# Seven half products for eight in the gate and up pairs of two SwiGLU layers, on one core

## The chip, the cores and the metric

The kernel runs on one core of one Trainium2 chip. The metric is device time in microseconds (us) of one execution, from the first to the last instruction and what lies around them. Lower is better. Times of the kernel before were taken in three runs.

## The reference, cut to what matters

A block of an encoder works on `x` of 256 rows and 2048 columns in float32: a feed-forward layer (FFN) added at half weight, then attention and retention side by side ("the mixer"), then a second FFN and a final norm.

```python
def swiglu_ffn(x, w_gate, w_up, w_down):
    return (jax.nn.silu(x @ w_gate) * (x @ w_up)) @ w_down
...
    x = x + 0.5 * swiglu_ffn(rmsnorm(x, norm_ffn1_g[l]), ffn1_w_gate[l], ffn1_w_up[l], ffn1_w_down[l])
    h = rmsnorm(x, norm_mix_g[l])
    proj = h @ w_in[l]
...
    x = x + merged @ w_out[l]
    x = x + 0.5 * swiglu_ffn(rmsnorm(x, norm_ffn2_g[l]), ffn2_w_gate[l], ffn2_w_up[l], ffn2_w_down[l])
return rmsnorm(x, norm_final_g)
```

The gate and up matrices are 2048 by 5632, the down matrix 5632 by 2048. Everything is wanted at nearly float32 precision.

## The kernel before, in words

**Precision by splitting.** TensorE multiplies a reduced float32 type (F32R). Each operand is therefore split into a high part, which is the value rounded to that type, and a low part, which is the rest. A product is three matmuls: high by high, high by low, low by high (lines 125 to 127). For weights the split is done on the chip as they arrive: ScalarE casts the tile to the high part (line 107), VectorE subtracts it from the raw tile to get the low part (line 108).

**Chunks.** All weights are read once, in chunks of 256 rows by 512 columns (two k-tiles of 128 rows, `KC = 2`, 512 KB). A chunk meets both row tiles of `x` (128 rows each), so it costs 2 k-tiles x 2 row tiles x 3 = 12 matmuls with 512 columns, one cast and one subtraction, both 128 partitions by 1024 elements. A block of 512 output columns is a `Gemm`: it has two accumulators in PSUM (one for each row tile), runs over its chunks, and at the end calls its `done` function, which takes the accumulators out. The whole kernel is one list of 768 chunks.

**The order.** `run` (line 129) walks the list. At step c it first calls `split_upto` (line 111), which issues the splits of up to a few chunks ahead (five tiles for the high part and five for the low part, `SPLIT_BUFS`), and with each split the load of a later chunk on SyncE's queue (four raw tiles). Then it issues what is due at this step, then the matmuls of chunk c. The order in which Python issues instructions is the order of each engine's queue; an engine does not pass an instruction that waits. So work that is issued behind a waiting instruction on the same engine waits too.

**The FFN** (line 366). There are 11 blocks of 512 columns. For each block the gate `Gemm` (8 chunks) is followed by the up `Gemm` (8 chunks). `gate_done` lets ScalarE apply silu (line 374), `up_done` lets VectorE multiply (line 379), and two steps later `put` transposes the product on TensorE (line 269, eight transposes) and splits it into high and low parts (lines 263 and 264). After six blocks, and again after the other five, the down products follow; `down_done` adds them to `x` on VectorE (line 357). The operand of gate and up is the transposed `x`, split by `Norm.put` (lines 316 to 333); the norm's factor is applied when the accumulators are taken out.

Of the kernel before, what the change touches and what calls it, by code (L numbers as in the profile page):

```python
# [32 lines left out]
SPLIT_BUFS = 5  # L33
ACT_TILES = 26
TAIL = 4
AHEAD = (2, 3)
WARM = (6, 3)
# [3 lines left out]
class Gemm:  # L41


    def __init__(self, w, row0, col0, nk, act, done):
        self.w, self.row0, self.col0, self.nk, self.act, self.done = w, row0, col0, nk, act, done
        self.parts = [(t, slice(0, NB)) for t in range(NT)]


@with_exitstack
def block_kernel(ctx: ExitStack, tc: tile.TileContext, x, g1, w1g, w1u, w1d, gm, w_in, rel, woa, wor, wo,  # L50
# [15 lines left out]
    def acc_tile(name):  # L66
        return psum.tile([P, NB], F32, tag="acc", name=name)

    def side_tile(name):
        return psum.tile([P, NB], F32, tag="side", name=name)  # L70
# [5 lines left out]
    chunks = []  # L76
    state = {"dma": 0, "split": 0, "step": 0}
    raws, splits = {}, {}
    due = {}

    def later(steps, fn):
        due.setdefault(state["step"] + steps, []).append(fn)

    def pieces(c):

        return [slice(j, j + 1) for j in range(KC)] if c == 0 else [slice(0, KC)]

    def load(c):
        job, k = chunks[c]
        t = wpool.tile([P, KC, NB], F32, tag="raw", bufs=RAW_BUFS, name=f"raw{c}")  # L90
        r0 = job.row0 + k * P
        src = job.w[r0 : r0 + KC * P, job.col0 : job.col0 + NB].rearrange("(k p) n -> p k n", p=P)
        for p in pieces(c):
            nc.sync.dma_start(t[:, p, :], src[:, p, :])
        raws[c] = t

    def load_next():
        if state["dma"] < len(chunks):
            load(state["dma"])
            state["dma"] += 1  # L100

    def split(c):
        raw = raws.pop(c)
        hi = wpool.tile([P, KC, NB], F32R, tag="hi", bufs=SPLIT_BUFS, name=f"hi{c}")
        lo = wpool.tile([P, KC, NB], F32R, tag="lo", bufs=SPLIT_BUFS, name=f"lo{c}")
        for p in pieces(c):
            nc.scalar.copy(hi[:, p, :], raw[:, p, :])  # L107
            nc.vector.tensor_sub(lo[:, p, :], raw[:, p, :], hi[:, p, :].bitcast(F32))  # L108
        splits[c] = hi, lo

    def split_upto(n):

        while state["split"] < min(len(chunks), n):
            while state["dma"] < min(len(chunks), state["split"] + RAW_BUFS):
                load_next()
            split(state["split"])
            state["split"] += 1
            load_next()

    def products(job, k, whi, wlo, part):  # L120
        ahi, alo = job.act(k)
        t, cs = job.parts[part]
        ts = slice(t * P, (t + 1) * P)
        acc, first, last = job.acc[part], k == 0, k == job.nk - 1
        nc.tensor.matmul(acc, ahi[:, ts], whi[:, cs], start=first, stop=False)  # L125
        nc.tensor.matmul(acc, ahi[:, ts], wlo[:, cs], start=False, stop=False)  # L126
        nc.tensor.matmul(acc, alo[:, ts], whi[:, cs], start=False, stop=last)  # L127

    def run(tail_done):
        head = len(chunks) - TAIL  # L130
        for c in range(head):
            state["step"] = c
            split_upto(c + min(SPLIT_BUFS, AHEAD[0] + c // AHEAD[1]) if c else 2)
            for fn in due.pop(c, []):
                fn()
            job, k0 = chunks[c]
            if k0 == 0:
                if job is chunks[-1][0]:
                    job.parts = TAIL_PARTS
                job.acc = [acc_tile(f"acc{c}_{t}") for t in range(NT)]  # L140
                job.acc += [side_tile(f"acc{c}_{t}") for t in range(NT, len(job.parts))]
                job.acc = [a[:, : cs.stop - cs.start] for a, (t, cs) in zip(job.acc, job.parts)]
            whi, wlo = splits.pop(c)
            for j in range(KC):
                for part in range(len(job.parts)):
                    products(job, k0 + j, whi[:, j, :], wlo[:, j, :], part)
            if k0 + KC == job.nk:
                job.done(job.acc)

        split_upto(len(chunks))  # L150
# [3 lines left out]
        for part, (t, cs) in enumerate(TAIL_PARTS):  # L154
            for c in range(head, len(chunks)):
                job, k0 = chunks[c]
                whi, wlo = splits[c]
                for j in range(KC):
                    products(job, k0 + j, whi[:, j, :], wlo[:, j, :], part)
            tail_done(job.acc[part], t, cs)  # L160
# [111 lines left out]
    class Operand:  # L272
# [18 lines left out]
        def __call__(self, k):  # L291
            return self.hi[k // 4][:, k % 4, :], self.lo[k // 4][:, k % 4, :]

    class Norm:


        def __init__(self, name, gain):
            self.name = name
            self.op = Operand(name, D // NB)
# [34 lines left out]

        def scale(self, t):
            return self.rstd[:, t : t + 1]

    def x_updated(norm):


# [7 lines left out]
    def add(jobs):  # L348
        for job in jobs:
            for k in range(0, job.nk, KC):  # L350
                chunks.append((job, k))
# [431 lines left out]
```

## Time and profile before

| | |
|---|---|
| median of three runs | 2179.64 us (2179.56 to 2180.44) |
| the profiled execution, whole | 2180.46 us |
| its span, first to last instruction | 2178.4 us |
| mean granted clock of TensorE | 0.999 |
| moved by DMA | 414.51 MB, mean 190 GB/s |

The profile is one execution. "Busy" of an engine is the time in which at least one of its instructions was under way. The lines of the profile name the kernel's line, the engine (PE is TensorE, PEld its weight load, DVE is VectorE, ACT is ScalarE, POOL is GpSimd, SP is SyncE), the operation, what is written from what, and shapes. A line of the grouped view ends with the total and mean duration and with the idle time of that engine just before these instructions and who ended it. In the view in order of time a line starts with the start and the duration in us; several like instructions in a row are one line with their count, and its duration is from the start of the first to the end of the last.

### The profile page before, as it was taken

What the parts mean: (1) busy time and instruction counts of PE and PEld (TensorE: products, weight loads), DVE (VectorE), ACT (ScalarE), POOL (GpSimd) and SP (SyncE); (2) the same over time, 40 slices, a digit from 0 to 9 for tenths busy, and PEclk for the clock granted to TensorE, in tenths of its full rate; (3) what the DMA queues carried; (4) which work ended last, traced back from release to release, by engine and by line L of the source; (5) the groups of instructions that cost most, each with busy time, mean ns of one, the idle gap of its engine ahead of it and who ended that gap; (6) DMA issues with size and microseconds to landing.
All of it is one profiled execution on the core that took longest, in us unless ns stands there. A gap on an engine that the chain in (4) does not pass through costs nothing.

```text
span 2178.4 us, 25308 instructions
## 1 busy us (share of the span) xinstructions
PE 2167.7 (100%) x9865; PEld 1802.5 (83%) x9865; DVE 1121.6 (51%) x1192; ACT 963.0 (44%) x1104; POOL 21.6 (1%) x36
## 2 busy tenths in 40 slices
PE   9999999999999999999999999999999999999998
PEld 7888888888888888888888888888888888888887
DVE  5544554445545544556655555554544544444554
ACT  6444433444444444454444444454444433444443
POOL 0000000000000000000000000000000000000000
PEclk9999999999999999999999999999999999999999
DMA  7655655666665555555555555556656556666554
GB/s 253 208 188 187 222 192 194 212 188 190 187 209 184 184 190 187 175 163 178 167 177 190 188 192 192 185 183 194 193 184 193 189 194 212 189 192 191 186 192 137
DMA packets 213512, 414.51 MB, mean 190 GB/s; under 512 B 12864, under 2 KB 13616, under 8 KB 213392
## 3 DMA queue, kind: packets, MB, share of 16 engines
q1 hardware_dynamic: 211424, 406.90, 57.9%
q0 software_dynamic: 1824, 5.93, 0.9%
q8 instruction: 77, 1.26, 0.2%
q14 instruction: 43, 0.35, 0.0%
q10 hardware_dynamic: 144, 0.07, 0.0%
HBM read 409.17 MB, written 3.67 MB: 190 GB/s over the span
## 4 chain that ended last, share of the span: by engine, by line
PE 99%; issue 0%; DMA 0%; ACT 0%; DVE 0%; POOL 0%; POOLq 0%; ACTq 0%
PE acc L125 32%; PE acc L126 32%; PE acc L127 32%; PE f2a0p L269 0%; PE f1a0p L269 0%; PE n1p L322 0%; DMA grows<-in_norm_ffn_g_dram 0%; PE f2a6p L269 0%; PE f1a6p L269 0%; PE mgp L269 0%; PE nmp L322 0%; PE n2p L322 0%; PE as L479 0%; PE rs L537 0%; PE av L514 0%
## 5 line engine op out<-in xcount | busy, mean ns | idle before, releaser
L108 DVE TENSOR_TENSOR lo<-raw,hi 128x1024 fp32r<-128x1024 f32 (+1 forms) x769 | 938.8, 1223 | 1014.0 <-ACT hi L107 1013.6
L107 ACT CAST hi<-raw 128x1024 fp32r<-128x1024 f32 (+1 forms) x769 | 808.2, 1052 | 1106.8 <-PE acc L127 1081.8
L125 PE MATMUL acc<-hi,nmh 128*128 128x512 f32 x704 | 277.8, 395 | 0.0
L125 PE MATMUL acc<-hi,n1h 128*128 128x512 f32 x704 | 276.2, 392 | 0.0
L125 PE MATMUL acc<-hi,n2h 128*128 128x512 f32 x704 | 274.8, 390 | 0.0
L126 PE MATMUL acc<-lo,n1h 128*128 128x512 f32 x704 | 274.7, 390 | 0.0
L127 PE MATMUL acc<-hi,n1l 128*128 128x512 f32 x704 | 274.6, 390 | 0.0
L127 PE MATMUL acc<-hi,nml 128*128 128x512 f32 x704 | 274.5, 390 | 0.0
L126 PE MATMUL acc<-lo,nmh 128*128 128x512 f32 x704 | 274.1, 389 | 0.0
L127 PE MATMUL acc<-hi,n2l 128*128 128x512 f32 x704 | 274.0, 389 | 0.0
L126 PE MATMUL acc<-lo,n2h 128*128 128x512 f32 x704 | 273.9, 389 | 0.0
L127 PEld LDWEIGHTS acc<-hi,n1l 128*128 128x128 f32 x704 | 132.4, 188 | 27.6
L127 PEld LDWEIGHTS acc<-hi,nml 128*128 128x128 f32 x704 | 132.2, 188 | 27.9
L125 PEld LDWEIGHTS acc<-hi,n1h 128*128 128x128 f32 x704 | 132.6, 188 | 27.3
L126 PEld LDWEIGHTS acc<-lo,n1h 128*128 128x128 f32 x704 | 132.4, 188 | 27.3 <-DVE lo L108 0.4
L127 PEld LDWEIGHTS acc<-hi,n2l 128*128 128x128 f32 x704 | 132.2, 188 | 27.5
L126 PEld LDWEIGHTS acc<-lo,n2h 128*128 128x128 f32 x704 | 132.2, 188 | 27.1
L125 PEld LDWEIGHTS acc<-hi,n2h 128*128 128x128 f32 x704 | 132.2, 188 | 27.0
L126 PEld LDWEIGHTS acc<-lo,nmh 128*128 128x128 f32 x704 | 132.3, 188 | 26.2
L125 PEld LDWEIGHTS acc<-hi,nmh 128*128 128x128 f32 x704 | 132.3, 188 | 26.2
L125 PE MATMUL acc<-hi,f2a0h 128*128 128x512 f32 x192 | 74.8, 390 | 0.0
L125 PE MATMUL acc<-hi,f1a0h 128*128 128x512 f32 x192 | 74.8, 389 | 0.0
(266 smaller groups left out, 2107.3 us busy)
## 6 DMA issues: line engine op xcount, KB each, us to landing
raw<-in_ffn_w_up_dram SPq DMA_DIRECT2D x176, 512.0 KB, 3.5
raw<-in_ffn_w_down_dram SPq DMA_DIRECT2D x176, 512.0 KB, 3.6
raw<-in_w_in_dram SPq DMA_DIRECT2D x176, 512.0 KB, 3.5
raw<-in_ffn_w_gate_dram SPq DMA_DIRECT2D x175, 512.0 KB, 3.5
raw<-in_w_out_dram SPq DMA_DIRECT2D x32, 512.0 KB, 3.7
raw<-in_w_out_att_dram SPq DMA_DIRECT2D x16, 512.0 KB, 4.3
raw<-in_w_out_ret_dram SPq DMA_DIRECT2D x16, 512.0 KB, 4.3
xall<-in_x_dram SPq DMA_DIRECT2D x3, 512.0 KB, 7.5
```

What stands on the lines that cost most here:

```text
L107: nc.scalar.copy(hi[:, p, :], raw[:, p, :])
L108: nc.vector.tensor_sub(lo[:, p, :], raw[:, p, :], hi[:, p, :].bitcast(F32))
L125: nc.tensor.matmul(acc, ahi[:, ts], whi[:, cs], start=first, stop=False)
L126: nc.tensor.matmul(acc, ahi[:, ts], wlo[:, cs], start=False, stop=False)
L127: nc.tensor.matmul(acc, alo[:, ts], whi[:, cs], start=False, stop=last)
```

## The change

In both FFNs block 0 stays as it was. For blocks 1 to 10 gate and up are taken as one product of 2 x 2 blocks: `x` is cut into two row tiles (t = 0, 1) and two halves of its columns (8 k-tiles each), and the weights into gate and up, each in the same two halves of rows. The plain way takes eight half products (2 row tiles x 2 column halves x 2 matrices) of 8 k-tiles x 3 = 24 matmuls. The change uses Strassen's scheme in Winograd's form: seven half products, some of them of sums of operands.

The sums of `x` (four, called s3, s5, s6, s7) are made once for each norm, on VectorE, and split like the rest (`add_up`). The sums of weights are made as the weights arrive, on VectorE, in place. A group (one gate and up pair) has 16 steps in four phases of four; a step takes 256 rows of a half:

- phase 0 (p steps): load gate and up of half 0; one sum; two splits; 12 matmuls, into banks a and c;
- phase 1 (q steps): load up of half 1; one sum; two splits; 12 matmuls, into a (with the sum first) and c;
- phase 2 (r steps): load gate of half 1; two sums; two splits; 12 matmuls, into a (with the sum first) and b;
- phase 3 (s steps): no load; one split (of the last sum); 6 matmuls, into a.

Bank a is read out between phases while it goes on accumulating. At the end of phase 0 ScalarE copies a and c; at the end of phase 1 it copies a, and VectorE adds c to that copy; at the end of phase 2 VectorE adds a and b to the copies of phase 0, ScalarE applies silu and VectorE multiplies; at the end of phase 3 ScalarE applies silu to a, and VectorE multiplies.

Between the steps stand plain chunks ("D"), eight in a group and thirteen in the last: up of block 0, then down products, which now run two blocks at a time. The order of a group is `WOVEN`. Eight plain chunks (gate of block 0) stand before the first group and eleven behind the last. Tiles for high and low parts become four each; a p, q or r step takes two of them, an s step or a plain chunk one, and a step is issued ahead only while four suffice. Loads of gate and up of half 0 go into eight tiles of their own (`KEPT`).

The diff, cut to its core:

```diff
 RAW_BUFS = 4
-SPLIT_BUFS = 5
-ACT_TILES = 26
-TAIL = 4
+SPLIT_BUFS = 4
+KEPT = 8
+ACT_TILES = 30
+TAIL = 2
 AHEAD = (2, 3)
+BY_DMA = ()
+HALF_K = D // P // 2
+LEAD = 8
+EARLY = 3
+WOVEN = "ppppD" "ppDppD" "pDpDpDpD" "ssssD"
+WOVEN_LAST = "pDppDpD" "pDpDpDpD" "pDpDpDpD" "ssDssD"
...
+    def prep_upto(n, c):
+
+        while state["prep"] < min(len(steps), n):
+            s = steps[state["prep"]]
+            if s.slots > state["slots"]:
+                return
+            load_some()
...
+            state["slots"] -= s.slots
+            s.prep()
+            for ring in s.frees:
+                room[ring] += 1
+            state["prep"] += 1
+            load_some()
...
         for c in range(head):
             state["step"] = c
-            split_upto(c + min(SPLIT_BUFS, AHEAD[0] + c // AHEAD[1]) if c else 2)
+            prep_upto(c + min(SPLIT_BUFS, AHEAD[0] + c // AHEAD[1]) if c else 2, c)
             for fn in due.pop(c, []):
                 fn()
...
+            steps[c].products()
+            state["slots"] += steps[c].slots
...
+        def add_up(self, p, n):
+
+            if n == 0:
...
+                s5, s7, s6, s3 = self.f
+                nc.vector.tensor_sub(s5, a22, a21)
+                nc.vector.tensor_sub(s7, a11, a21)
+                nc.vector.scalar_tensor_tensor(s6, s5, -1.0, a11, op0=ALU.mult, op1=ALU.subtract)
+                nc.vector.scalar_tensor_tensor(s3, s6, -1.0, a12, op0=ALU.mult, op1=ALU.subtract)
+            for i in (2 * n, 2 * n + 1):
+                self.split_to(self.SUMS[i], slice(4 * p, 4 * p + 4), self.f[i])
...
+            def two(first, second):
+
+                tiles = []
+                for i, raw in enumerate((first, second)):
+                    hi = wpool.tile([P, KC, NB], F32R, tag="hi", bufs=SPLIT_BUFS, name=f"hi{name}{i}")
+                    lo = wpool.tile([P, KC, NB], F32R, tag="lo", bufs=SPLIT_BUFS, name=f"lo{name}{i}")
+                    nc.scalar.copy(hi, raw)
+                    tiles.append((raw, hi, lo))
+                for raw, hi, lo in tiles:
+                    nc.vector.tensor_sub(lo, raw, hi.bitcast(F32))
+                return [(hi, lo) for _, hi, lo in tiles]
+
+            def prep():
+                x = self.x[jc]
+                if phase == 0:
+                    if "T1" not in BY_DMA:
+                        nc.vector.tensor_add(x, x, self.kept[jc])
+                    made["w"] = two(self.kept[jc], x)
+                elif phase == 1:
+                    raw = made["raw"]
+                    if "T2" not in BY_DMA:
+                        nc.vector.tensor_add(x, x, raw)
+                    made["w"] = two(raw, x)
+                elif phase == 2:
+                    raw, k = made.pop("raw"), self.kept.pop(jc)
+                    nc.vector.tensor_sub(k, x, k)
...
+                        nc.vector.tensor_add(x, x, raw)
+                    made["w"] = two(raw, k)
+                else:
+                    made["w"] = [split(self.x.pop(jc), name)]
+
+            def products():
+                w = made["w"]
+                if phase == 0:
+                    self.product("a", "a00", jc, w[0], True, False)
+                    self.product("c", "s5", jc, w[1], True, False)
+                elif phase == 1:
+                    self.product("a", "s6", jc, w[1], False, False)
+                    self.product("c", "s3", jc, w[0], False, True)
+                elif phase == 2:
+                    self.product("a", "s7", jc, w[1], False, False)
+                    self.product("b", "a01", jc, w[0], True, True)
+                else:
+                    self.product("a", "a11", jc, w[0], False, True)
+                if jc == n - 1:
+                    self.end(phase)
...
+            if phase == 0:
+                copied("s1", "a", norm.scale(0))
+                copied("s5", "c", norm.minus_scale(1))
+            elif phase == 1:
+                copied("s2", "a", norm.minus_scale(0))
+                r = copy["s2"]
+                nc.vector.scalar_tensor_tensor(r, acc["c"], norm.minus_scale(0), r, op0=ALU.mult, op1=ALU.add)
+                self.evict(0, 1, r)
+            elif phase == 2:
+                r = copy["s5"]
+                nc.vector.scalar_tensor_tensor(r, acc["a"], norm.minus_scale(1), r, op0=ALU.mult, op1=ALU.add)
+                self.evict(1, 1, r)
+                r = copy["s1"]
+                nc.vector.scalar_tensor_tensor(r, acc["b"], norm.scale(0), r, op0=ALU.mult, op1=ALU.add)
+                self.evict(0, 0, r)
+            else:
+                self.evict(1, 0, None, acc["a"])
...
+            def evict(t, side, r, acc=None):
+                if side == 1:
+                    got["up", t] = r
+                    return
+                if acc is not None:
+                    r = tmp_tile(f"{name}h{b}{t}", "scaled", 2)
+                    nc.scalar.activation(r, acc, AF.Silu, scale=norm.scale(t))
+                else:
+                    nc.scalar.activation(r, r, AF.Silu)
+                nc.vector.tensor_mul(r, r, got.pop(("up", t)))
+                got[t] = r
+                if 0 in got and 1 in got:
+                    later(2, lambda: put_mid(b, got))
```

`copied` is an activation of ScalarE that copies a bank of PSUM to SBUF with the norm's factor; `three` issues the three matmuls of one product; `split` is the cast and the subtraction of before; `room` counts free raw and kept tiles, and `load_some` issues loads in order while the next one has room.

More of the change, by code (lines that the diff above doesn't have):

```diff
@@ L77, in block_kernel @@
-    state = {"dma": 0, "split": 0, "step": 0}
-    raws, splits = {}, {}
+    steps = []
+    transfers = []
+    state = {"dma": 0, "prep": 0, "step": 0}
+    room = {"raw": RAW_BUFS, "kept": KEPT}
     due = {}
[L81 to L93, printed above, removed]
-            nc.sync.dma_start(t[:, p, :], src[:, p, :])
-        raws[c] = t
@@ L108, in split @@
             nc.vector.tensor_sub(lo[:, p, :], raw[:, p, :], hi[:, p, :].bitcast(F32))
[L109 to L127, printed above, removed]
+        return hi, lo
```

339 lines of the change are left out of this document (249 added, 90 removed).

## The prediction

> **What bounds the kernel now.** First the page: busy times, the clock row and the chain that ended last.
>
> ```profile
> PE 2167.7 (100%) x9865; PEld 1802.5 (83%) x9865; DVE 1121.6 (51%) x1192; ACT 963.0 (44%) x1104; POOL 21.6 (1%) x36
> ...
> PEclk9999999999999999999999999999999999999999
> ...
> PE 99%; issue 0%; DMA 0%; ACT 0%; DVE 0%; POOL 0%; POOLq 0%; ACTq 0%
> ```
>
> TensorE (PE) is never without work and makes up 99% of the chain. So what counts is how far its instructions stand apart, and which engine would be next. Second, the groups by line, for who waits for whom:
>
> ```profile
> L108 DVE TENSOR_TENSOR lo<-raw,hi 128x1024 fp32r<-128x1024 f32 (+1 forms) x769 | 938.8, 1223 | 1014.0 <-ACT hi L107 1013.6
> L107 ACT CAST hi<-raw 128x1024 fp32r<-128x1024 f32 (+1 forms) x769 | 808.2, 1052 | 1106.8 <-PE acc L127 1081.8
> ```
>
> ScalarE's cast waits for TensorE to give back a tile, VectorE's subtraction for the cast: both run behind TensorE with slack. Third, the order of time around 303 us (ScalarE, then VectorE), and one pair's stretch with its transposes:
>
> ```profile
> 302.77 1.05 ACT L107 CAST hi<-raw 128x1024 fp32r<-128x1024 f32 x1 [1.67 <-PE acc L127]
> 305.49 1.05 ACT L107 CAST hi<-raw 128x1024 fp32r<-128x1024 f32 x1 [1.67 <-PE acc L127]
> ```
> ```profile
> 303.86 1.22 DVE L108 TENSOR_TENSOR lo<-raw,hi 128x1024 fp32r<-128x1024 f32 x1 [1.50 <-ACT hi L107]
> 306.58 1.22 DVE L108 TENSOR_TENSOR lo<-raw,hi 128x1024 fp32r<-128x1024 f32 x1 [1.50 <-ACT hi L107]
> ```
> ```profile
> 149.53:193.94 44.41, 44.41 (x202) 36.86 (x201) 22.12 (x20) 19.10 (x20) 0.00 (x0) 1.00 0.60 190
> ```
> ```profile
> 149.53 0.87 PE f1a0p L269 x8
> 193.94 0.87 PE f1a0p L269 x8
> ```
>
> One chunk passes every 305.49 - 302.77 = 2.72 us. That is 12 matmuls, so one takes 0.2267 us. The third block is a row of busy times by stretch (length, then busy time and count of PE, PEld, VectorE, ScalarE and POOL, clock, DMA share and rate), the fourth two lines of the chain. A pair of 16 chunks takes 16 x 2.72 + 0.87 (eight transposes) = 44.39 us, and the row says 44.41. In it VectorE is busy 22.12 us, half. The hop from ScalarE to VectorE is 303.86 - (302.77 + 1.05) = 0.04 us.
>
> **What VectorE and ScalarE take when they are not idle.** The change sends VectorE more than it has slack for, so I need the spacing of its instructions back to back. Five rows of the order of time, VectorE first:
>
> ```profile
> 38.77 4.63 DVE L108 TENSOR_TENSOR lo<-raw,hi 128x1024 fp32r<-128x1024 f32 x4 [3.15 <-ACT hi L107]
> ...
> 56.66 1.40 DVE L379 SCALAR_TENSOR_TENSOR f1g<-acc,n1rstd,f1g 128x512 f32<-128x512 f32 x2
> ```
> ```profile
> 313.16 1.28 DVE L357 SCALAR_TENSOR_TENSOR xall<-acc,xall 128x512 f32<-128x512 f32 x2
> ```
> ```profile
> 1151.85 0.69 DVE L613 TENSOR_TENSOR sigr<-sigr,siga 128x512 f32<-128x512 f32 x1
> 1152.46 0.68 DVE L612 TENSOR_TENSOR sigr<-acc,sigr 128x512 f32<-128x512 f32 x1
> ```
> ```profile
> 37.69 2.95 ACT L107 CAST hi<-raw 128x1024 fp32r<-128x1024 f32 x3
> ```
> ```profile
> 213.24 1.37 ACT L374 ACTIVATE f1g<-acc,n1rstd 128x512 f32<-128x512 f32 x2 [0.98 <-PE acc L127]
> ```
>
> Four subtractions of 1024 elements: (4.63 - 1.22) / 3 = 1.137 us apart, each done 1.22 us after its start. With 512 elements: 0.61 us (1152.46 - 1151.85); the x update about 0.60 (half of 1.28, less the overlap); the form with a scale per row 0.66 (1.40 less about 0.74 for the last). Casts of 1024 stand (2.95 - 1.05) / 2 = 0.95 apart; the copy of a bank takes about 0.69. The trace has no float32 sum of 1024 elements from SBUF to SBUF. The add at line 613 is that operation at 512 and has the spacing of its neighbours, so I take 1.137 for the sums, with 1.22 (nothing overlaps) as the upper bound and nothing below it, since 1024 / 512 of 0.61 is already 1.22.
>
> The Trainium skill ("VectorE: DVE Perf Modes", "The DRAIN you can't avoid") has it that the next VectorE instruction does not start until the pipe of the one before is empty; by that every instruction would cost its full 1.22 us, and the sum below is 4.5 us a group more (a rival, below). The same section says that an instruction that is not held starts earlier, and with that this trace agrees: 1.137 against 1.22.
>
> **The sum for one regular group** (16 steps and 8 plain chunks), of which each FFN has nine. Before, the same work is 24 chunks: 24 x 2.72 + 0.87 = 66.2 us.
>
> *TensorE.* Seven half products of 24 matmuls and 8 x 12: 264 x 0.2267 + 0.87 = 60.7 us. It gains 24 x 0.2267 = 5.4 us, in all 20 groups 109 us, if it stays the bound.
>
> *VectorE.* A p or q step has one sum and two subtractions, an r step two and two, an s step one subtraction, a plain chunk one: 8 x 3 + 4 x 4 + 4 + 8 = 52 instructions x 1.137 = 59.1 us. Small ones: three with a scale at ends of phases (2.0), two silu multiplies (1.2), two x updates for each of two down blocks (2.4), two subtractions behind the transposes (1.2): 6.8 us. Together 65.9 us. So VectorE becomes the bound, with as much work as the group took before. The best this can do is to leave the time as it was.
>
> *Where VectorE's queue stands still.* With four tiles, the next step can be split only while TensorE works on the present one, and TensorE begins a step just when VectorE has finished it. The waits that follow, with a step of 2.72 us:
> - p and q steps: sum done at 1.22, hop 0.04, cast 1.05, hop 0.04 = 2.35, while VectorE has two instructions, 2.27. Eight times 0.08 = 0.7 us.
> - End of phase 0: the copies of banks a and c are issued ahead of the casts of the first q step. The last p step ends about 1.5 us after VectorE left it (its second half is 6 x 0.2267 = 1.36 and starts with VectorE's last result); the copies take 1.37, the cast 1.05, the hops 0.1: 4.0 us, against two instructions in hand (2.3). Wait 1.7 us.
> - End of phase 1: VectorE's add of bank c comes behind the last q step (2.72), the copy of a (0.69) and hops (0.1): 3.5 us, and it has one instruction to do in that time (1.14). Wait 2.4 us. Behind it the first r step's four instructions are queued, and TensorE has only one plain chunk (2.72) for the 6 us from its last q step to the first r step's operands (0.7 + 0.1 + 0.66 + 4 x 1.14): it stands still some 3 us. In the middle of this phase one cast waits for a step to end, 0.4 us.
> - End of phase 2: two instructions in hand (2.27) against a step and a hop (2.8): 0.5 us. The multiply comes right behind the silu of ScalarE: 0.1 (the add's own end) + 0.69 + 0.1 (hops) = 0.9 us. The next cast is behind the silu: 0.4 us.
> - End of phase 3: nothing; VectorE is behind by then (five short steps), and TensorE, not VectorE, has the slack.
>
> Sum 7.0 us. A regular group takes 65.9 + 7.0 = 72.9 us, 6.7 more than before. Between the ends (0, if the queue is never late; 9.7, if every wait is 40% longer) I take the worked value, as each step of it has a row.
>
> *The last group* has 13 plain chunks. Before: 29 x 2.72 + 0.87 = 79.8. After: TensorE 324 x 0.2267 + 0.87 = 74.3, VectorE 57 x 1.137 + 8.0 = 72.8 and some 4 of waits: 77. It gains 2.8 us.
>
> *The rest.* Eight plain chunks before and eleven behind the groups cost as before. At the start and before the second FFN VectorE makes the sums of x and splits them, 16 x 0.61 = 9.8 us more, ScalarE about as much:
>
> ```profile
> 0.00:50.00 50.00, 47.09 (x213) 39.33 (x214) 27.42 (x37) 33.42 (x56) 2.46 (x9) 1.00 0.75 255
> ```
>
> VectorE and ScalarE have 23 and 17 us free there; what is late costs perhaps 3 us each time (0 to 10): +6. The mixer and the tail keep their work. Loads:
>
> ```profile
> raw<-in_ffn_w_up_dram SPq DMA_DIRECT2D x176, 512.0 KB, 3.5
> ```
>
> They are as many as before, 24 in a longer group, and land in 3.5 us. The kept tiles come free from the first r step on, over 10 us before they are needed. I cost them at nothing; their cover is that lead, and without it a late load costs up to 3.5 us.
>
> Total, against the profiled execution (2180.5 us with what lies around its span, 0.8 above the median): 18 x 6.7 = +121, 2 x -2.8 = -6, +6: **2301 us**.
>
> **The rivals.**
>
> *The queue is never late (not slower).* If ScalarE and TensorE always answer before VectorE asks, a group takes VectorE's 65.9: 18 x -0.3 - 2 x 5.5 (TensorE's 74.3 in the last groups) + 6 = -10, so 2170 us. It decides at 0.3 us of waits a group. For it: every s step and plain chunk gives VectorE time to get ahead. Against it: four tiles are two steps, and three phase ends put a wait on TensorE's last matmul into VectorE's queue.
>
> *TensorE stays the bound.* 18 x -5.5 - 11 + 6 = -104: 2076 us. It needs (60.7 - 6.8) / 52 = 1.04 us for an instruction of VectorE; the x4 row says 1.137.
>
> *Nothing overlaps on VectorE.* If each instruction started only when the one before is done, 52 x (1.223 - 1.137) = 4.5 us a group and 4.9 in the last: +90, 2391 us. The x4 row speaks against it, unless sums are held where subtractions are not; line 613, which needs the result of the multiply just ahead of it, is the kind that could be.
>
> *The clock drops in the gaps.* The end of the trace shows it:
>
> ```profile
> 2170.00:2172.00 2.00, 0.62 (x6) 0.42 (x4) 1.06 (x3) 0.51 (x2) 0.00 (x0) 1.00 0.76 272
> 2172.00:2174.00 2.00, 0.00 (x0) 0.00 (x0) 0.88 (x2) 1.33 (x2) 0.55 (x1) 0.63 0.02 7
> 2174.00:2178.40 4.40, 0.00 (x0) 0.00 (x0) 0.00 (x0) 0.00 (x0) 0.00 (x0) 0.50 0.64 235
> ```
>
> The last matmul ends at 2170.6; a mean of 0.63 over two microseconds is full clock for 0.5 us and half clock after that, so it fell 1.9 us behind the last matmul. The gap before the first r step is about 3 us, and its step at half clock takes 5.4 instead of 2.7, with VectorE's next cast waiting for its end: 2.7 x 20 = +54, 2355 us. Against it: the other gaps are under 2 us, and how long the clock stays low is not seen. The Trainium skill ("TensorE: Matmul & The Clock Gate", Part 1) lets the clock fall after a whole idle window of about 3.4 us that runs free of the kernel; by that these gaps would keep the clock.
>
> **How the numbers follow.** The forecast (VectorE the bound, 4 to 10 us of waits a group) has 0.74, the clock 0.14, the queue never late 0.06, nothing overlaps 0.04, TensorE the bound 0.02. The forecast's own range is 18 x 2.7 = 49 us to each side, 2252 to 2350; with the clock's case the range is 2250 to 2360, which holds 8 in 10. A measurement of this kernel can tell about 0.2% (4 us) from no change. Faster takes TensorE's case and most of the late-free one, 0.06; the same 0.02; slower 0.92.
>
> **What would show it.** Right: the transposes of the FFN's products stand about 73 us apart; in the groups VectorE is busy about 90% and TensorE waits for L108-like subtractions; the waits of VectorE on the bank copies and on silu stand where I put them, with TensorE's longest gap before the first r step; sums of 1024 elements stand 1.14 us from the next instruction. Wrong: TensorE without gaps in the groups, groups of 61 to 66 us, sums closer than 1.04 us or as far apart as 1.22, a granted clock under 0.97, or casts that wait for loads.

## The result, and the profile after

The changed kernel took 2303.9 us (median of four runs, 2301.5 to 2305.2), the kernel before 2179.6 (2179.3 to 2180.4): 1.057 times the time, interval 1.055 to 1.0587. The profiled execution has a span of 2302.8 us, against 2178.4 before: 124.4 us more.

The page of the changed kernel: busy times, two rows of the 40 slices, the chain, two groups of lines.

```profile
PE 2146.3 (93%) x9337; PEld 1714.8 (74%) x9337; DVE 1836.1 (80%) x1910; ACT 1239.7 (54%) x1468; POOL 21.6 (1%) x36
...
DVE  5999999999999754555655555679999999999997
...
PEclk8999999999999999999999999999999999999999
...
PE 54%; DVE 27%; issue 7%; ACT 6%; DMA 6%; SPq 0%; ACTq 0%; DVEq 0%; POOL 0%; POOLq 0%
...
L115 DVE TENSOR_TENSOR lo<-raw,hi 128x1024 fp32r<-128x1024 f32 (+1 forms) x449 | 545.8, 1220 | 312.1 <-ACT hi L114 311.5
...
L501 DVE TENSOR_TENSOR loz<-rawz,hiz 128x1024 fp32r<-128x1024 f32 x160 | 195.1, 1219 | 22.4 <-ACT hiz L498 22.4
```

The row of slices tells the story. In both FFNs VectorE stands at nine tenths; in the mixer, which the change leaves alone, it is at four to six as before. In the chain VectorE now has 27% where it had nothing. The two groups show why: the plain subtraction (line 115) still had 312 us of idle time before it, nearly all of it in the mixer; the same subtraction in a Strassen step (line 501) had 22 in all. There the cast is ready before VectorE is.

Three groups as stretches (length, then busy time and count of PE, PEld, VectorE, ScalarE and POOL, clock, DMA share and rate), each from the first product into bank a to the next group's; and, as a check, four lines of the chain in order of time, the pair of x updates on which each group ends:

```profile
485.60:557.18 71.58, 65.40 (x275) 50.82 (x274) 67.23 (x65) 40.11 (x43) 0.00 (x0) 0.98 0.53 176
557.18:628.76 71.58, 65.40 (x275) 50.80 (x274) 67.25 (x65) 40.10 (x43) 0.00 (x0) 0.98 0.53 176
628.76:700.35 71.59, 64.10 (x276) 49.59 (x274) 67.25 (x64) 40.41 (x44) 1.52 (x2) 1.00 0.55 185
```

```profile
413.38 1.28 DVE xall L587 x2
484.98 1.28 DVE xall L587 x2
556.57 1.28 DVE xall L587 x2
628.15 1.28 DVE xall L587 x2
```

Both say 71.6 us a group, where the prediction had 72.9 and the work took 66.2 before. VectorE is busy 67.25 of the 71.58 and idle 4.33; TensorE's 264 products and 8 transposes would fit into 60.7.

Where the 124.4 us came from, by the first matmul of each part in the two traces: the 18 regular groups +104.2 (1298.2 us, against 1194.0 for the same 432 chunks before, 66.3 for 24 of them; most groups took 71.6, the first three 75.8, 74.0 and 73.5); the start until the first group +12.3; the same place in the second FFN 0.0; the two last groups with the eleven chunks behind them +3.7 and +1.2; the mixer +1.1; what lies behind the last matmul +1.9. The sum is 124.4.

Now VectorE in one group, in order of time (start, duration, instruction, and in brackets the idle time before it and who ended it):

```profile
570.76 1.22 DVE L513 TENSOR_TENSOR z176x<-z176x,rawz 128x1024 f32<-128x1024 f32 x1
572.99 1.23 DVE L501 TENSOR_TENSOR loz<-rawz,hiz 128x1024 fp32r<-128x1024 f32 x1 [1.01 <-ACT hiz L498]
...
575.26 1.22 DVE L513 TENSOR_TENSOR z176x<-z176x,rawz 128x1024 f32<-128x1024 f32 x1
576.40 1.22 DVE L501 TENSOR_TENSOR loz<-rawz,hiz 128x1024 fp32r<-128x1024 f32 x1
577.68 1.22 DVE L501 TENSOR_TENSOR loz<-z176x,hiz 128x1024 fp32r<-128x1024 f32 x1
...
587.08 1.22 DVE L115 TENSOR_TENSOR lo<-raw,hi 128x1024 fp32r<-128x1024 f32 x1
590.11 0.75 DVE L561 SCALAR_TENSOR_TENSOR z176s<-z176c,n1minus,z176s 128x512 f32<-128x512 f32 x1 [1.81 <-PE z176c L124]
590.78 1.22 DVE L517 TENSOR_TENSOR z176k<-z176x,z176k 128x1024 f32<-128x1024 f32 x1
592.03 1.22 DVE L521 TENSOR_TENSOR z176x<-z176x,rawz 128x1024 f32<-128x1024 f32 x1
...
618.50 0.69 DVE L636 TENSOR_TENSOR z176s<-z176s,z176s 128x512 f32<-128x512 f32 x1 [0.70 <-ACT z176s L635]
619.44 3.50 DVE L115 TENSOR_TENSOR loz<-z176x,hiz 128x1024 fp32r<-128x1024 f32 x3 [0.25 <-ACT hiz L114]
```

Every wait stands at the end of a phase: 1.01 us where phase 0's banks are copied ahead of the first q step's cast, 1.81 where phase 1's bank c is added, 0.70 and 0.25 around the silu. Between the sum at 575.26 and the next instruction lie 1.14 us, the spacing that the prediction took from the subtractions. Between line 517 and line 521 lie 1.25: the second sum of an r step overwrites a tile (z176x) that the first one reads, and it starts only when that one is done.

TensorE around the first r step of that group, and at the kernel's start:

```profile
593.18 0.50 PE L122 MATMUL z176a<-hiz,n1s7h 128*128 128x512 f32 x1 [0.47 <-ACT hiz L498]
595.58 0.50 PE L123 MATMUL z176a<-loz,n1s7h 128*128 128x512 f32 x1 [1.89 <-DVE loz L501]
```

```profile
36.37 1.09 PE L386 MATMUL n1p<-id_sb,xall 128*128 128x128 f32 x4 [8.84 <-DMA xall<-in_x_dram]
```

TensorE's gap before the r steps is there, cut in two by one matmul, which needs only the high part and was ready early. The 8.84 us at the start are new: a transpose waits for the last quarter of `x`.

### The profile page after: what moved, and what is told of

It is laid out like the page before. It is cut to its first block, busy times and chain, and to the rows that moved or that the text cites. A ratio compares the mean times of both kernels' runs of the same rounds, so it can differ in the third digit from the quotient of the medians.

```text
span 2302.8 us, 25403 instructions
## 1 busy us (share of the span) xinstructions
PE 2146.3 (93%) x9337; PEld 1714.8 (74%) x9337; DVE 1836.1 (80%) x1910; ACT 1239.7 (54%) x1468; POOL 21.6 (1%) x36
## 4 chain that ended last, share of the span: by engine, by line
PE 54%; DVE 27%; issue 7%; ACT 6%; DMA 6%; SPq 0%; ACTq 0%; DVEq 0%; POOL 0%; POOLq 0%
PE acc L122 12%; PE acc L123 12%; PE acc L124 12%; DVE loz L501 8%; ACT hiz L498 4%; DVE lo L115 3%; DVE xall L587 2%; DMA raw<-in_ffn_w_down_dram 2%; DVE loz L115 1%; DMA xall<-in_x_dram 1%; DMA z536x<-in_ffn_w_up_dram 0%; DMA rawz<-in_ffn_w_up_dram 0%; ACT hi L114 0%; PE z8a L123 0%; SPq L108 0%
## 5 line engine op out<-in xcount | busy, mean ns | idle before, releaser
L115 DVE TENSOR_TENSOR lo<-raw,hi 128x1024 fp32r<-128x1024 f32 (+1 forms) x449 | 545.8, 1220 | 312.1 <-ACT hi L114 311.5
L114 ACT CAST hi<-raw 128x1024 fp32r<-128x1024 f32 (+1 forms) x449 | 469.7, 1047 | 343.1 <-PE acc L124 312.6
L501 DVE TENSOR_TENSOR loz<-rawz,hiz 128x1024 fp32r<-128x1024 f32 x160 | 195.1, 1219 | 22.4 <-ACT hiz L498 22.4
L498 ACT CAST hiz<-rawz 128x1024 fp32r<-128x1024 f32 x160 | 167.1, 1045 | 55.3 <-issue 28.4
L122 PE MATMUL acc<-hi,nma00h 128*128 128x512 f32 x176 | 70.6, 401 | 0.0
L122 PE MATMUL acc<-hi,nma01h 128*128 128x512 f32 x176 | 70.1, 398 | 0.0
L124 PE MATMUL acc<-hi,nma00l 128*128 128x512 f32 x176 | 68.7, 390 | 0.0
L124 PE MATMUL acc<-hi,nma01l 128*128 128x512 f32 x176 | 68.6, 390 | 0.0
L122 PE MATMUL acc<-hi,nma10h 128*128 128x512 f32 x176 | 68.6, 390 | 0.0
L123 PE MATMUL acc<-lo,nma00h 128*128 128x512 f32 x176 | 68.6, 390 | 0.0
```

The lines of the kernel that those rows point to most:

```text
L122: nc.tensor.matmul(acc, ahi, whi, start=first, stop=False, **more)
L123: nc.tensor.matmul(acc, ahi, wlo, start=False, stop=False, **more)
L124: nc.tensor.matmul(acc, alo, whi, start=False, stop=last, **more)
L498: nc.scalar.copy(hi, raw)
L501: nc.vector.tensor_sub(lo, raw, hi.bitcast(F32))
```

## The experiments

The theory: a group takes VectorE's own work, 65.9 us, and the waits that the ends of phases put into its queue; what is left of the loss arises at the start, where a load is late. Rivals: the loss comes from the clock, from late loads within the groups, or from the order of the steps rather than from VectorE's load.

**e1: without the sums of weights.** All 16 sums of a group are left out.

```diff
-                        nc.vector.tensor_add(x, x, self.kept[jc])
+                        pass
...
-                        nc.vector.tensor_add(x, x, raw)
+                        pass
...
-                    nc.vector.tensor_sub(k, x, k)
...
-                        nc.vector.tensor_add(x, x, raw)
+                        pass
```

> The sixteen sums of weight tiles of each group are left out (VectorE issues none of them; the products then use the plain tiles, so the result is not the reference's). Theory (VectorE is the bound, 52 x 1.137 + 6.8 + 5.7 of waits = 71.6 us a group as measured): VectorE's work falls to 36 x 1.137 + 6.8 = 47.7 us, under TensorE's 60.7, and a group takes 61 to 65 us, somewhat over 60.7 because four tiles still allow only two steps ahead. The whole: 2304 - 20 x 6.6 to 10.6 = 2090 to 2170 us. Rival (the four tiles, the bank copies and the order of the steps hold TensorE up, and VectorE only looks busy): the group stays at 68 us or more, the whole over 2230 us.

Measured: 2140.5 us, 0.9823 of before (0.9808 to 0.9837). One group as a stretch:

```profile
434.78:497.55 62.77, 61.59 (x275) 50.23 (x273) 49.62 (x48) 41.02 (x44) 0.00 (x0) 1.00 0.61 201
```

The group fell by 8.8 us to 62.8, 163 us over the kernel. TensorE is busy 61.59 of it, so it is the bound again; steps, order and banks are as they were. The sums are shown to be the cause. Leaving them out also spares a cast the wait for its sum, but the rows of the changed kernel put that wait at 0.14 us a step (577.68 - 576.40 = 1.28 us, less 1.14), and VectorE at 67.25 us of work in 71.58; it is the time of the sums that counts. The run also shows what is left of TensorE's 109 us in this order of steps, with the start as it is, even if the sums were free: 39.

**e2: the end of a phase one step later.** The copies and adds at a phase's end are issued one step later, so that VectorE meets them when the banks are done.

```diff
-                    self.end(phase)
+                    later(1, lambda: self.end(phase))
```

> The end of each phase (bank copies, adds of banks, silu, multiply) is issued one step later, behind the splits that are issued at that step and ahead of the next step's matmuls. Nothing is left out. Theory (these ends put waits into VectorE's queue, 1.0 us at the end of phase 0, 1.9 at phase 1, 1.2 at phase 2): about 3 to 4 us a group go, 60 to 80 us in all: 2225 to 2245 us. Rival (VectorE's work alone sets the group, and its waits come back elsewhere, at the tiles): 2290 us or more.

Measured: 2257.8 us, 1.0361 (1.0345 to 1.0376). One group, and VectorE where it had waited 1.81 us:

```profile
470.43:539.71 69.28, 63.80 (x274) 49.63 (x272) 67.27 (x64) 40.25 (x44) 0.00 (x0) 1.00 0.56 182
```

```profile
506.08 1.22 DVE L115 TENSOR_TENSOR lo<-raw,hi 128x1024 fp32r<-128x1024 f32 x1
507.22 0.75 DVE L561 SCALAR_TENSOR_TENSOR z152s<-z152c,n1minus,z152s 128x512 f32<-128x512 f32 x1
507.88 1.22 DVE L517 TENSOR_TENSOR z152k<-z152x,z152k 128x1024 f32<-128x1024 f32 x1
```

The wait at the end of phase 1 is gone. A group is 2.3 us shorter, less than I expected: the two waits that it could remove held 1.01 + 1.81 = 2.8 us, and VectorE's own work did not shrink (busy 67.27, as before the edit). So these waits are shown to be some two fifths of the 5.4 us that a group had lost; with them gone VectorE is still busy for 67.27 of 69.28 us.

**e3: the last quarter of x loaded first.** In the changed kernel it is issued at step 2, behind loads of weights that `load_some` may issue much further ahead now.

```diff
     load_x(2 * NB, 3 * NB)
+    load_x(3 * NB, 4 * NB)
...
-    at(2, lambda: load_x(3 * NB, 4 * NB))
```

> The load of the last quarter of x is issued at the start, before the weight loads of the first group, and not at step 2 behind eight of them. Nothing is left out. Theory (TensorE's gap of 9.0 us at 27 us of the profile is that load, queued behind 4 MB of weights): 8 to 12 us less, 2292 to 2296 us. Rival (the gap is the late sums of x, and would only move): under 3 us less.

Measured: 2295.3 us, 1.0532 (1.0515 to 1.055): 8.6 us less, with groups as long as before (71.56). The transposes of the last quarter now follow without a gap:

```profile
26.80 0.60 PE L386 MATMUL n1p<-id_sb,xall 128*128 128x128 f32 x4
...
31.05 0.60 PE L386 MATMUL n1p<-id_sb,xall 128*128 128x128 f32 x4
```

**e8: e2 and e3 together.**

> Both of the earlier edits together: the ends of the phases one step later, and the last quarter of x loaded first. Nothing is left out. Theory: they act at different places (in the groups, before the groups) and add up: 2304 - 46 - 9 = 2249 us (2245 to 2253). Rival (x first only moves the start, and the group's waits come back): 2258 us or more.

Measured: 2253.2 us, 1.0339 (1.0322 to 1.0356), a group of 69.28. The two edits nearly add: 2303.9 - 46.1 - 8.6 = 2249.2, 4 us below the measurement. With both, 74 us of loss are left, 18 x 3.1 = 56 of them in the regular groups, where VectorE is all but full. The next six runs try to give that work to somebody else.

**e4: three of four sums by DMA.** The kernel has a switch, `BY_DMA`, that lets a DMA on GpSimd's queue add one tile to another.

```diff
-BY_DMA = ()
+BY_DMA = ("T1", "T2", "T4")
```

> Twelve of the sixteen sums of weight tiles of a group are made by accumulating DMAs that GpSimd issues, four stay on VectorE. Nothing is left out. Theory (VectorE is the bound): VectorE's work falls by 12 x 1.137 = 13.6 us to 52.3, TensorE's 60.7 is the bound if the DMAs are in time, a group takes 61 to 66 us, the whole 2090 to 2190 us, about the kernel before or under it. Rival (a sum of 512 KB by DMA takes too long or takes the engines of the loads away, 53% busy now): TensorE waits for sums, the group is longer than 71.6 us, the whole over 2304 us.

Measured: 2481.9 us, 1.1402 (1.1371 to 1.1434). One group; GpSimd's queue; VectorE behind it:

```profile
548.16:629.84 81.68, 68.16 (x275) 53.29 (x274) 53.81 (x52) 40.43 (x44) 10.30 (x12) 0.90 0.85 229
```

```profile
693.52 0.86 POOL L478 DMA_DIRECT2D z200x<-z200k  x1 [12.15 <-DMA z200x<-in_ffn_w_up_dram]
694.10 1.16 POOL L519 DMA_DIRECT2D z176x<-rawz  x1
...
705.92 1.22 DVE L115 TENSOR_TENSOR loz<-z176x,hiz 128x1024 fp32r<-128x1024 f32 x1 [11.15 <-ACT hiz L114]
```

VectorE's busy time fell to 53.8 us of a group, and the group still became 10 longer. Line 478, the sum of the *next* group's p step (z200), waited 12.15 us for its weights; the sum that this group's s step needs (line 519, z176) stood behind it in the same queue, and VectorE then waited 11.15 us, for a cast that waited for that sum. An engine's queue is as much a resource as its time. The DMA share rose from 0.53 to 0.85 besides, and the granted clock fell to 0.90; what each of these cost was not separated.

**e9: one of four sums by DMA**, the second sum of an r step, on top of e8.

```diff
-BY_DMA = ()
+BY_DMA = ("T4",)
```

> As the kernel before in this list, with the second sum of each r step made by an accumulating DMA issued by GpSimd (four of sixteen; it is needed only in the s steps). Nothing is left out. Theory (VectorE's work sets the group; the twelve sums by DMA failed because sums with a short deadline came late and blocked the queue for the others): four instructions of 1.137 us less, a group 69.3 - 4.5 = 64.8 us, the whole 2249 - 90 = 2159 us (2150 to 2185), under the kernel before. Rival (accumulating DMAs hinder VectorE or the loads whatever their deadline): 2249 us or more.

Measured: 2220.2 us, 1.019 (1.0173 to 1.0208), 33 less than e8. One group, then ScalarE and VectorE at one point of it:

```profile
523.25:590.76 67.51, 62.88 (x273) 49.85 (x272) 62.34 (x59) 39.78 (x44) 3.39 (x4) 1.00 0.72 215
```

```profile
576.00 1.05 ACT L114 CAST hi<-raw 128x1024 fp32r<-128x1024 f32 x1 [2.46 <-DMA raw<-in_ffn_w_down_dram]
```

```profile
577.08 1.23 DVE L115 TENSOR_TENSOR lo<-raw,hi 128x1024 fp32r<-128x1024 f32 x1 [2.28 <-ACT hi L114]
```

VectorE lost 5 us of work (62.34 instead of 67.27), and the group got 1.8 shorter. The rest went to waits that had not been there, two of VectorE's for a cast, 3.2 us together: the DMA share is 0.72, and one cast waited 2.46 us for a load of `w_down`. So the run lies between the theory and its rival.

**e10: two of four sums by DMA**, the sum of the p step as well, issued at most three steps ahead so that it does not block the queue.

```diff
-BY_DMA = ("T4",)
+BY_DMA = ("T1", "T4")
...
-                if "T1" in BY_DMA:
-                    nc.gpsimd.dma_start(self.x[jc], self.kept[jc], accum_op=ALU.add)
...
+            def sum_first():
+                if jc not in self.x:
+                    return False
+                nc.gpsimd.dma_start(self.x[jc], self.kept[jc], accum_op=ALU.add)
+                return True
...
-                        early if phase == 1 and "T2" in BY_DMA else None)
+                        sum_first if phase == 0 else None)
```

> As the kernel before in this list, with the sum of the p steps by an accumulating DMA as well, issued up to three steps ahead (eight of sixteen). Nothing is left out. Theory: VectorE has 56.8 us of work, the group falls to the 62.7 us that it took without any sum, the whole to 2249 - 20 x 6.6 = 2117 us (2110 to 2150). Rival (a sum by DMA takes 7 us and p steps follow every 3 us, one queue does them in turn): p steps wait, the whole is longer than with one sum by DMA by 20 us or more.

Measured: 2311.2 us, 1.0604 (1.0584 to 1.0624). One group, the chain, and a cast of ScalarE:

```profile
626.48:698.91 72.43, 65.60 (x273) 51.63 (x272) 58.05 (x55) 40.23 (x43) 5.99 (x7) 0.95 0.82 233
```

```profile
PE 51%; DMA 28%; DVE 9%; ACT 5%; issue 4%; SPq 1%; ACTq 0%; POOLq 0%; POOL 0%; DVEq 0%
```

```profile
641.98 1.04 ACT L496 CAST hiz<-z200x 128x1024 fp32r<-128x1024 f32 x1 [5.22 <-DMA z200x<-z200k]
```

VectorE is down to 58 us of a group and 9% of the chain, and DMA has 28%, where the changed kernel has 6. As the rival had it, the p steps wait: in this group casts waited 10.9 us for sums by DMA, and another 4.8 for loads. The bound has moved on to the transfers.

**e5: one of four sums on GpSimd**, the second sum of an r step, in the changed kernel as it is.

```diff
-                        nc.vector.tensor_add(x, x, raw)
+                        nc.gpsimd.tensor_add(x, x, raw)
```

> The second sum of each r step (needed only in the s steps, many us later) is made by GpSimd and not by VectorE; all else as changed. Nothing is left out. Theory (VectorE's work sets the group): four instructions of 1.137 us leave VectorE's queue, a group falls from 71.6 to about 67 us, the whole to 2304 - 20 x 4.5 = 2214 us (2205 to 2235). Rival (GpSimd and VectorE hinder each other): VectorE's instructions get longer while GpSimd adds, the group falls by under 2 us or grows, the whole 2265 us or more. The price of such a sum on GpSimd is in no trace so far.

Measured: 2377.0 us, 1.0908 (1.0892 to 1.0925). GpSimd and VectorE at the same time:

```profile
638.80 3.26 POOL L521 TENSOR_TENSOR z176x<-z176x,rawz 128x1024 f32<-128x1024 f32 x1 [3.49 <-issue]
```

```profile
638.59 1.21 DVE L501 TENSOR_TENSOR loz<-rawz,hiz 128x1024 fp32r<-128x1024 f32 x1
639.86 3.28 DVE L501 TENSOR_TENSOR loz<-z176k,hiz 128x1024 fp32r<-128x1024 f32 x1
643.07 1.21 DVE L115 TENSOR_TENSOR lo<-raw,hi 128x1024 fp32r<-128x1024 f32 x1
```

The subtraction that starts at 639.86 takes 3.28 us instead of 1.21 and ends 1.08 after GpSimd's sum does (642.06). It reads as though VectorE stood still until GpSimd was done. So a sum on GpSimd saves VectorE 1.137 us and costs it 2.07 (the other three of this group 2.06, 1.84 and 2.06): four of them should make a group 3.7 us longer, and 73.1 us more in 20 groups is 3.7. The Trainium skill ("SBUF — State Buffer", "Who interferes with whom") has it that a VectorE instruction with two SBUF inputs contends with a GpSimd instruction that reads SBUF, that the lock on the ports they share is exclusive, and that the order of issue decides which of the two is blocked; the rows agree.

**e6 and e7: two and three sums on GpSimd**, on e8, the p step's (and for e7 the q step's) sum issued up to three steps ahead.

```diff
-                        nc.vector.tensor_add(x, x, self.kept[jc])
+                        pass
...
-                        nc.vector.tensor_add(x, x, raw)
+                        nc.gpsimd.tensor_add(x, x, raw)
...
+            def sum_first():
+                if jc not in self.x:
+                    return False
+                nc.gpsimd.tensor_add(self.x[jc], self.x[jc], self.kept[jc])
+                return True
...
+            ahead = {0: sum_first}
...
-                        early if phase == 1 and "T2" in BY_DMA else None)
+                        ahead.get(phase))
```

> The sum of the p steps (issued up to three steps ahead) and the second sum of the r steps on GpSimd, the ends of the phases issued one step later, and the last quarter of x loaded first. Nothing is left out. Theory: VectorE has 65.9 - 9.1 = 56.8 us of work and some 3.4 of waits, under the 62.7 that a group took without any sum, which then is the bound: 2140 less 9 for the load of x, 2130 us (2120 to 2155), faster than both kernels. Rival (GpSimd too slow for eight sums a group, or it slows VectorE): 2200 us or more.

> As the kernel before in this list, with the sum of the q steps on GpSimd too (twelve of sixteen). Nothing is left out. Theory: VectorE was no longer the bound there, so this changes little: 2120 to 2150 us. Rival (each sum on GpSimd costs more than it spares, since the step waits for it): longer than the kernel with two sums by 20 us or more.

Measured: 2436.3 us (1.1175, interval 1.1158 to 1.1192) and 2496.6 (1.1462, 1.1443 to 1.1481). By e5's price, 8 and 12 sums of 0.93 us net in 20 groups on e8's 2253, I get 2402 and 2476; the runs are 34 and 21 above that, and where those go was not followed. Both times are those of the rival.

**e11: six pairs instead of ten.** If VectorE's work is the bound, the remedy is more plain chunks beside each Strassen group: a plain chunk takes TensorE 2.72 us and VectorE 1.14. Blocks 1, 3, 5, 7, 9 and 10 go by Strassen, with 16 plain chunks in each group, and 8 (ahead of the first two), 16 (ahead of the next three) or none (ahead of the last) before it; e2's and e3's edits are in, and a product is transposed one step earlier.

```diff
-                    later(2, lambda: put_mid(b, got))
+                    later(1, lambda: put_mid(b, got))
...
+        STRASSEN = (1, 3, 5, 7, 9, 10)
+        WOVEN_PAIR = "pDpDpDpD" "pDpDpDpD" "pDDpDDpDDpD" "ssssD"
+        WOVEN_END = "ppDpDpDD" "pDpDpDpD" "pDDpDDpDDpD" "ssssD"
-        queue = plain(0)
+        queue = plain(0) + plain(2)
...
+            if 2 * pair + 4 < nblocks - 1:
+                queue += plain(2 * pair + 4)
...
-        next_standard(LEAD)
-        for b in range(1, nblocks):
+        before = {1: LEAD, 3: 8, 5: 16, 7: 16, 9: 16, 10: 0}
+        for b in STRASSEN:
+            next_standard(before[b])
...
-    at(mix - 24, set_bias)
-    at(mix - 16, set_decay)
+    at(mix - 6, set_bias)
+    at(mix - 4, set_decay)
...
-    at(len(steps) - 60, final_gain)
+    at(len(steps) - 30, final_gain)
```

> Six of eleven pairs of each FFN by the seven products (blocks 1, 3, 5, 7, 9, 10), each with sixteen plain chunks woven in, so that VectorE gets fewer instructions for each of TensorE's; the other pairs plain; ends of the phases one step later, the last quarter of x loaded first. All sums on VectorE, nothing left out. Theory (VectorE's work sets the time, nothing else about the scheme costs): a woven group has 60 x 1.137 + 9 = 77 us of VectorE's work and 360 x 0.2267 + 0.9 = 82.5 us of TensorE's, so TensorE is the bound, each pair saves 5.4 us: 2180 - 12 x 5.4 + 5 (sums of x, ends) = 2120 us (2110 to 2145), faster than both kernels. Rival (a step that needs two tiles waits whatever VectorE has to do, and the banks read between phases cost): 2 to 5 us a group stay as waits, 2150 to 2190 us.

Measured: 2153.0 us, 0.988 (0.9864 to 0.9897): faster than both kernels. One cycle, a group with its 16 plain chunks inside and 16 behind it:

```profile
282.19:410.00 127.81, 127.37 (x569) 105.19 (x568) 101.56 (x96) 68.99 (x71) 0.00 (x0) 1.00 0.62 196
```

TensorE is busy 127.37 of 127.81 us: its 552 matmuls and 16 transposes make 552 x 0.2267 + 1.74 = 126.9. VectorE has 26 us to spare. TensorE is the bound, and Strassen's gain is kept but for 0.9 us.

**e12: the same, with 16 plain chunks ahead of the first group** and none behind it, and two tables of the mixer made after its start instead of before it.

```diff
-        before = {1: LEAD, 3: 8, 5: 16, 7: 16, 9: 16, 10: 0}
+        before = {1: 2 * LEAD, 3: 0, 5: 16, 7: 16, 9: 16, 10: 0}
...
-    at(mix - 6, set_bias)
-    at(mix - 4, set_decay)
+    at(mix + 10, set_bias)
+    at(mix + 14, set_decay)
```

> As the kernel with six pairs, with sixteen plain chunks ahead of the first woven group in place of eight (eight fewer behind it), and the tables of the attention loaded sixteen to eighteen steps later, within the mixer. Nothing is left out. Theory (in the profile with six pairs TensorE stands still about 6 us ahead of the first group, while the sums of x are made, and 4 us at the end of the first FFN behind the transposes of the bias table): both go, 8 to 12 us less, 2141 to 2145 us. Rival (the sums of x and the tables take VectorE and ScalarE as long wherever they stand): 2150 us or more.

Measured: 2147.2 us (2146.4 to 2147.9), 0.9853 (0.9836 to 0.9869), the fastest version here; 5.7 us better than e11, less than I had expected. TensorE's two waits that the edit aimed at (4.9 and 4.1 us in e11) are down to 0.7 together, but a new one of 2.3 has come, put down to a copy of the gains on VectorE (line 231). Its page:

```profile
PE 2112.9 (99%) x9529; PEld 1744.5 (81%) x9529; DVE 1573.8 (73%) x1662; ACT 1153.1 (54%) x1348; POOL 21.6 (1%) x36
...
PE 92%; DVE 3%; ACT 3%; issue 1%; DMA 0%; POOL 0%; ACTq 0%; POOLq 0%; DVEq 0%
```

TensorE's busy time fell by 2167.7 - 2112.9 = 54.8 us, and 21 of that came back as idle time (31.7 instead of 10.7 within the span).

## Why the prediction was right, and where its terms were off

The mechanism was the one forecast, and 2301.0 us stands beside 2303.9. But the terms agree less well than the total. The groups came out 17 us below their term, the start, the last groups, the mixer and the end together some 20 above theirs. That these nearly cancel is luck.

**VectorE's work: right.** 52 instructions at 1.137 us and 6.8 of small ones, 65.9 a group. The sums of float32, which no row of before showed, stand 1.14 from the next instruction unless that one is held. e1 shows what they decide.

**The waits: 5.7 us a group instead of 7.0** (71.6 less 65.9), -23 over 18 groups. Part of that, 8.6 us, came back in the first FFN's first three groups: VectorE is busy there 69.4, 68.7 and 68.4 us with the last sums of `x`, block 0's multiply and transposes, and a table of the mixer, and idle 6.4, 5.4 and 5.1 instead of 4.3. By the sum of the groups (+104.2, where I had +121) the term was 17 too large. Of my terms the end of phase 0 was 1.0 (predicted 1.7), that of phase 1 was 1.8 (2.4, and the 0.4 in mid-phase was not there), the silu 0.7 and 0.25 (0.9 and 0.4), the end of phase 2 nothing of TensorE's (0.5). The p and q steps cost 0.14 each instead of 0.08, and the held second sum of four r steps another 0.45, which I had not named. Most places were right and most sizes too large.

**The last groups: wrong by 10 us.** I gave each -2.8; with what follows them they came to +3.7 and +1.2. I had counted the work and guessed "some 4" for the waits; which wait it is was not followed.

**The loads: wrong, and the step that failed.** "I cost them at nothing; their cover is that lead" holds within the groups: in neither FFN's groups is a wait put down to a load of weights. (The chain's 6% of DMA do not say otherwise: a load can stand in the chain that landed while VectorE was at work, as one at 621.73 us did, inside the run of three subtractions that starts at 619.44.) At the start there is no lead. The eight `KEPT` tiles are free, so eight more loads (4 MB) can go onto SyncE's queue ahead of the last quarter of `x`, and TensorE stands for 8.84 us. I gave the start and the passage to the second FFN +6 together; they took 12.3 and 0.0. e3 gives 8.6 back. The load of `x` did not move, but others were let past it; going through SyncE's queue load by load would have found that.

**The rivals.** "The queue is never late" and "TensorE stays the bound" are both refuted by the rows of waits and by the 67.25 us of VectorE. "Nothing overlaps" is refuted by the spacing of 1.14, except for an instruction that is held by the one before it (1.25). The clock did drop, and this is the interesting one. Two stretches of 3.41 us in the second group above, and the same two in the third:

```profile
593.62:597.03 3.41, 1.52 (x7) 1.24 (x7) 3.41 (x4) 1.41 (x2) 0.00 (x0) 1.00 0.42 102
597.03:600.45 3.42, 3.42 (x9) 2.63 (x8) 3.39 (x4) 2.04 (x2) 0.00 (x0) 0.50 0.59 204
665.30:668.72 3.42, 1.55 (x7) 1.31 (x8) 3.42 (x4) 1.31 (x2) 0.00 (x0) 1.00 0.39 113
668.72:672.13 3.41, 3.41 (x17) 2.83 (x16) 3.38 (x4) 2.00 (x2) 0.00 (x0) 1.00 0.57 192
```

In the second group TensorE ran at half clock for 3.4 us, in the third it did not. But the second (mean clock 0.98) took 71.58 us and the third (1.00) 71.59: TensorE has some 10 us of slack in a group, so here the price was nothing. The rival named a real event and forgot that the engine it slows was no longer the bound.

Why in one group and not in its neighbour, the trace does show. Every change of the granted clock in it stands on a grid of 3.413 us. With each matmul counted as 0.227 us, all 15 stretches of the grid behind which the clock fell were at most 0.39 full, and all those at full clock behind which it stayed were at least 0.41 full. (In the other runs' traces the border lies between 0.38 and 0.47 by this count and is less sharp; what the chip itself counts is not shown.) From 310.3 us to 597.0 it falls five times, 71.68 us apart, which is 21 of the grid's steps; the groups take 71.58, so the gap before the r steps slides against the grid by 0.1 us a group, until the stretch that holds it is full enough (1.52 us of work above, then 1.55).

What stays open: the 34 and 21 us in e6 and e7, the last groups' waits, and what the low clock cost in the first three groups, where its mean is 0.93 to 0.95.

## What to carry to other kernels

A scheme that trades TensorE's products for sums is worth what the engine that makes the sums has free in that stage: count that engine's instructions at their spacing first, and apply the scheme only as often as the time that is free allows (with e2's and e3's edits in both, six pairs of eleven gained 1.2%, and 1.5% in e12; ten lost 3.4%). Work moved off a bound engine isn't free because the other engine is idle: it may share a port (GpSimd), a queue (e4) or bandwidth (e9, e10) with something on the path. When buffers are added, look at the start of the kernel for the load that the new ones are let past.

## What the runs showed of the hardware that was not expected

- A float32 sum of 128x1024 on GpSimd took 3.26 us beside VectorE and made one subtraction of VectorE take 3.28 instead of 1.21.
- A VectorE sum of 128x1024 that overwrites a tile which the sum ahead of it reads started 1.25 us after that one; others started after 1.14.
- A sum from SBUF to SBUF by an accumulating DMA is a large load on the DMA engines: four tiles of 512 KB in a group raised the share from 0.56 to 0.72, eight to 0.82.
- The clock fell to half behind a stretch of 3.41 us with 1.52 of work, after two gaps of 0.47 and 1.89 us with one matmul between them, and stayed up behind one with 1.55. The Trainium skill ("TensorE: Matmul & The Clock Gate", Part 1) asks for a whole idle window of about 3.4 us; the idle stretches here were shorter, and by the measurement they sufficed in some groups and not in others.
